# A decoder block with mLSTM and DeltaNet: all mLSTM queries and keys by seven-product blocks, DeltaNet columns projected in front, and mixer units of 40 steps

## The chip, the cores and the metric

The kernel runs on one core of a Trainium2 chip. The metric is the time of one execution on the device in microseconds (us), the median of three runs. Engines are called as the profile calls them: PE is TensorE (matrix products; PEld its weight loads), DVE VectorE, ACT ScalarE, POOL GpSimd, and SP SyncE, which here only issues DMAs.

## The reference

One layer on x of 512 rows and 2048 columns, float32. The input is normalised, one wide projection makes everything, two token mixers run side by side, and an output projection with a gated merge closes the layer:

```python
u = _rmsnorm(h, norm_w)
proj = jnp.matmul(u, w_in)            # to ml_q, ml_k, ml_v, ml_o, ml_z, ml_i, ml_f,
                                      # dn_qkv, dn_z, dn_b, dn_a, gate_a, gate_b
# mLSTM: 8 heads, query/key width 128, value width 256, chunkwise
h_a = _merge_heads(_rmsnorm(_mlstm_chunkwise(q, k, v, i_pre, logf))) * ml_norm_w
h_a = h_a * sigmoid(ml_o) * silu(ml_z)
# gated DeltaNet: 16 heads of 128; causal conv of 4 taps + SiLU on q, k, v
qkv = _causal_conv_silu(dn_qkv, dn_conv_w)
h_b = _merge_heads(_rmsnorm(_gated_delta_chunkwise(l2norm(dq), l2norm(dk), dv, beta, g), dn_norm_w)) * silu(dn_z)
y = sigmoid(gate_a) * (h_a @ w_out[:2048]) + sigmoid(gate_b) * (h_b @ w_out[2048:])
out = _rmsnorm(x + y)

# a chunk of DeltaNet, state S, gam the running sum of the log decay g
u = wv - wk @ S                       # wv, wk: solved from (I + strict(beta k k^T decay))
o = (q * exp(gam)) @ S + (q k^T * decay) @ u
S = exp(gam_end) * S + (k * exp(gam_end - gam))^T @ u
```

## The kernel before

Everything is float32. For a large product each operand is split in two reduced parts: ACT casts the upper part (`split_hi`, L140) and DVE subtracts it from the value (`split_lo`, L143). A product is then three matmuls: upper by upper, lower by upper, upper by lower (L257 to L259, L578 to L580). A weight tile is loaded by SP (`load_raw`, four buffers `wr`) and split into `wh` and `wl` (four buffers each).

PE's order is written by hand: instructions stand on each engine in the order in which the program issues them, moved only by the marks `urgent` (ahead) and `behind` (right after the newest split of that engine). The measure of progress is the step: after each group of six large matmuls `tick()` (L219) is called, and it resumes each of the generators that are due. A generator issues a piece of the mixers' work and gives back the number of steps after which it wants to go on (`yield 2`); `start(gen, wait)` sets its first step. So all times in the plan are counted in steps, not in us.

The stages are:

1. Front: the norm of x, its transposed split `uh`, `ul` in SBUF, gates, and four direct blocks (`proj_cm`, L246): 256 output columns, 16 row tiles, 96 matmuls, 16 steps. They make queries and keys of the first four mLSTM heads, which go to DRAM (`spill`).
2. The seven-product stage (`seven_stage`, L480): blocks of two times 512 columns by seven products of half size in place of eight, 336 matmuls each. Each block has half A (8 steps of four products) and half B (8 of three), where a product is a step. For a block DVE and ACT also form sums of weight tiles (L519, L520, L538) and split these. The list `SEVEN` has 13 blocks: mLSTM z and o gates, DeltaNet's gate, one block with the other four heads' queries and keys, mLSTM values, and the merge gates.
3. Eight mixer units (`dn_unit`, L1128) of 48 steps, two DeltaNet heads each. In a unit three direct blocks make the columns of keys, values and queries; each has a convolution (L828 to L837), SiLU (L843, L844) and a turn to token order (L860). Beside them run DeltaNet's generators: `dn_front_k` (key products and the decay matrix `dm`, L887, L898), `dn_front_q` (L985), `dn_back` (the triangular solve) and `dn_chain` (the recurrence over four chunks: pr, r, pw, w, pst, st, L1079 to L1102), and one mLSTM head (`ml_head`, L1161) whose first step is in `HEADS`.
4. The output projection: direct wide blocks, two seven-product blocks, a last block, and the final norm.

In `dn_chain` the value enters as v times beta (`vn` multiplied by `nk` on DVE, L1029), and the first product of a chunk, keys by state, is scaled by the negated decay `negeg` when r is formed:

```python
V.scalar_tensor_tensor(out=r, in0=pr, scalar=negeg[:, c, h:h + 1], in1=vn[:, c, :], op0=ALU.mult, op1=ALU.add)
```

The queries get the decay `eg` (in the tile `gb`) on POOL in `dn_front_q` (L995).

## Time and profile before

| | |
|---|---|
| median of three runs (lowest, highest) | 2144.73 us (2144.39, 2144.76) |
| the profiled execution, its span | 2143.23 us, 2141.5 us |
| mean granted TensorE clock | 0.998 |
| busy: PE, DVE, ACT, POOL | 99%, 80%, 49%, 21% |
| front with its four direct blocks | to 124 us |
| 13 seven-product blocks | 124 to 1115 us, some 76 us each |
| eight units | 1115 to some 1800 us, some 86 us each in the middle |
| output projection and final norm | the rest |

The span runs from the first to the last instruction. A busy PE is one that has a matmul in it; since matmuls are pipelined, a matmul's own length (0.39 us) is longer than the distance to the next. The line numbers (L257) are those of the kernel before.

### The profile page before, as it was taken

Reading aid. Unit: us, or ns where it says so; the run is one execution under the profiler, and the core shown is the slowest. Engines: PE = TensorE matmul, PEld = TensorE weight load, DVE = VectorE, ACT = ScalarE, POOL = GpSimd, SP = SyncE. Lnnn points to the kernel's source line nnn. Section 1 sums busy time; section 2 is a strip of 40 time slices with the busy share of each in tenths; the row PEclk is TensorE's granted clock in tenths of the full one; section 3 lists DMA queues with packets and bytes.
Section 4 is the critical chain, followed back from the end, with each engine's and each line's share of the span. In section 5 each row is a group of like instructions: output and inputs, shape, how many; then the busy total and the mean of one; then the engine's idle time right before and its main releaser. Section 6 shows DMA issues by size and latency. Waiting matters only on the chain.

```text
span 2141.5 us, 32018 instructions
## 1 busy us (share of the span) xinstructions
PE 2113.5 (99%) x10544; PEld 1752.6 (82%) x10544; DVE 1708.0 (80%) x2981; ACT 1057.6 (49%) x2066; POOL 451.1 (21%) x667
## 2 busy tenths in 40 slices
PE   6999999999999999999999999999999999999998
PEld 5888888888888888888888888888888888887886
DVE  5888888788788778777766887888878878569887
ACT  5444454445444444444445546456465464345345
POOL 0000000000004000000003335344343363233211
PEclk9999999999999999999999999999999999999999
DMA  5355676667677767766766867777686677778895
GB/s 162 119 192 190 212 217 198 220 199 224 206 234 237 245 196 226 240 209 212 253 205 165 208 166 180 183 180 192 182 211 173 171 189 224 196 223 287 245 302 225
DMA packets 447144, 444.21 MB, mean 207 GB/s; under 512 B 197121, under 2 KB 303842, under 8 KB 446850
## 3 DMA queue, kind: packets, MB, share of 16 engines
q1 hardware_dynamic: 377618, 337.22, 53.9%
q0 software_dynamic: 24752, 72.90, 10.9%
q10 hardware_dynamic: 44608, 32.06, 4.8%
q8 instruction: 82, 1.34, 0.3%
q14 instruction: 84, 0.69, 0.1%
HBM read 348.66 MB, written 97.58 MB: 208 GB/s over the span
## 4 chain that ended last, share of the span: by engine, by line
PE 95%; DVE 2%; DMA 2%; issue 1%; SPq 0%; POOL 0%; ACT 0%; DVEq 0%; POOLq 0%; ACTq 0%
PE ps L578 18%; PE ps L580 18%; PE ps L579 18%; PE pj L257 10%; PE pj L259 9%; PE pj L258 9%; PE py L1407 2%; PE py L1409 2%; PE py L1408 2%; PE pk L915 1%; DMA wr<-in_w_out_dram 1%; PE pqk L990 1%; PE pw L1087 1%; PE pnum L1213 1%; PE po L1102 1%
## 5 line engine op out<-in xcount | busy, mean ns | idle before, releaser
L143 DVE TENSOR_TENSOR wl<-wr,wh 128x512 fp32r<-128x512 f32 (+1 forms) x522 | 444.3, 852 | 176.5 <-ACT wh L140 172.3
L140 ACT CAST wh<-wr 128x512 fp32r<-128x512 f32 (+1 forms) x522 | 373.9, 717 | 422.1 <-PE pj L258 218.5
L257 PE MATMUL pj<-uh,wh 128*128 128x512 f32 x896 | 375.8, 419 | 0.0
L259 PE MATMUL pj<-uh,wl 128*128 128x512 f32 x896 | 351.5, 392 | 0.0
L258 PE MATMUL pj<-ul,wh 128*128 128x512 f32 x896 | 349.8, 390 | 0.0
L578 PE MATMUL ps<-wh,uh 128*128 128x512 f32 x752 | 292.7, 389 | 0.8 <-DVE X L632 0.8
L579 PE MATMUL ps<-wl,uh 128*128 128x512 f32 x752 | 292.6, 389 | 0.0
L580 PE MATMUL ps<-wh,ul 128*128 128x512 f32 x752 | 292.6, 389 | 0.0
L140 ACT CAST wh<-t 128x1024 fp32r<-128x1024 f32 x120 | 126.3, 1053 | 301.7 <-PE ps L580 197.5
L533 POOL DMA_DIRECT2D t_d<-ts x104 | 56.6, 544 | 921.8 <-DVE ts L520 853.5
L579 PE MATMUL ps<-wl,suh 128*128 128x512 f32 x624 | 242.9, 389 | 0.0
L580 PE MATMUL ps<-wh,sul 128*128 128x512 f32 x624 | 242.8, 389 | 0.0
L578 PE MATMUL ps<-wh,suh 128*128 128x512 f32 x624 | 242.8, 389 | 0.0
L140 ACT CAST wh<-ts 128x512 fp32r<-128x512 f32 x240 | 147.9, 616 | 184.7 <-DVE ts L538 157.6
L143 DVE TENSOR_TENSOR wl<-t,wh 128x1024 fp32r<-128x1024 f32 x120 | 147.0, 1225 | 81.9 <-ACT wh L140 81.5
L259 PEld LDWEIGHTS pj<-uh,wl 128*128 128x128 f32 x896 | 168.3, 188 | 37.0
L257 PEld LDWEIGHTS pj<-uh,wh 128*128 128x128 f32 x896 | 169.2, 189 | 29.7
L258 PEld LDWEIGHTS pj<-ul,wh 128*128 128x128 f32 x896 | 169.3, 189 | 28.5
L143 DVE TENSOR_TENSOR wl<-ts,wh 128x512 fp32r<-128x512 f32 x240 | 164.9, 687 | 32.6 <-ACT wh L140 31.2
L578 PEld LDWEIGHTS ps<-wh,uh 128*128 128x128 f32 x752 | 141.2, 188 | 30.4 <-DVE X L632 1.2
L579 PEld LDWEIGHTS ps<-wl,uh 128*128 128x128 f32 x752 | 141.2, 188 | 29.5
L580 PEld LDWEIGHTS ps<-wh,ul 128*128 128x128 f32 x752 | 141.2, 188 | 29.2
(345 smaller groups left out, 3804.2 us busy)
## 6 DMA issues: line engine op xcount, KB each, us to landing
wr<-in_w_in_dram SPq DMA_DIRECT2D x744, 256.0 KB, 3.6
wr<-in_w_out_dram SPq DMA_DIRECT2D x138, 256.0 KB, 4.8
t_d<-ts POOLq DMA_DIRECT2D x104, 256.0 KB, 3.6
wr<-t_d SPq DMA_DIRECT2D x104, 256.0 KB, 3.7
xt<-in_x_dram SPq DMA_DIRECT2D x8, 512.0 KB, 7.2
tg_d<-X ACTq DMA_DIRECT2D x16, 256.0 KB, 4.8
tg_d<-to ACTq DMA_DIRECT2D x16, 256.0 KB, 4.6
v<-v_d SPq DMA_DIRECT2D x8, 512.0 KB, 5.6
```

The costliest lines, as they stand in the source:

```text
L140: newest["A"] = A.copy(hi, src).ins
L143: newest["V"] = V.tensor_tensor(out=lo, in0=src, in1=hi.bitcast(F32), op=ALU.subtract).ins
L257: T.matmul(ps[j], hi[:, k, wsl], uh[:, kt, :], start=(kt == 0), stop=False)
L258: T.matmul(ps[j], hi[:, k, wsl], ul[:, kt, :], start=False, stop=False)
L259: T.matmul(ps[j], lo[:, k, wsl], uh[:, kt, :], start=False, stop=(kt == KT - 1))
L533: queue.dma_start(t2_d[b % 2, i], ts[:, 0, :])
L578: T.matmul(ps[t], ah, hi, start=(g == "A" and i == 0), stop=False, skip_group_check=True)
L579: T.matmul(ps[t], ah, lo, start=False, stop=False, skip_group_check=True)
L580: T.matmul(ps[t], al, hi, start=False, stop=(i == KH - 1), skip_group_check=True)
L1407: T.matmul(ps[c], uh[:, kt, tsl], hi, start=(kt == ks[0]), stop=False)
L1408: T.matmul(ps[c], uh[:, kt, tsl], lo, start=False, stop=False)
L1409: T.matmul(ps[c], ul[:, kt, tsl], hi, start=False, stop=(kt == ks[-1]))
```

## The change

The mLSTM queries and keys of all eight heads now come from two seven-product blocks (`SEVEN` has 14 blocks). The four direct blocks in front make DeltaNet columns instead: the keys of heads 0 and 1, and the values of the six odd heads 3 to 13, in pairs whose pieces of 128 columns lie 256 apart (kind "w", two DMAs per weight tile). Their raw results go to DRAM (`raw_d`). During the seven-product blocks 0 to 7, generators `before_mixers` read them back, one head each, and do convolution, SiLU and turn; the results go to DRAM once more (`pre_d`, `kc_d`).

So unit 0 has no key block (32 steps), units 1 to 6 project the values of one head only (`proj_half`, 8 steps; 40 in all), and unit 7 stays at 48: 320 steps in place of 384. `HEADS`, the waits of `dn_front_k` and `dn_back` and the start of `open_y` are set anew.

In DeltaNet, keys too are multiplied by `eg` on POOL after their own products are done; r is then formed in one instruction from v, beta and the product, and v is no more multiplied by beta ahead, but for chunk 0 (on ACT).

```diff
-HEADS = (1, 41, 85, 130, 178, 226, 274, 322)
+HEADS = (1, 37, 74, 111, 148, 186, 225, 264)
+PRE = (16, 17, 35, 37, 39, 41, 43, 45)
+VPRE = {(h - 33) // 2: i for i, h in enumerate(PRE) if h > 32}
 SEVEN = ([("z", ML_Z + c, ML_O + c) for c in range(0, D, NO)]
          + [("s", DN_Z + c, DN_Z + c + NO) for c in range(0, D, 2 * NO)]
-         + [("q", ML_Q + QKS, ML_K + QKS)]
+         + [("q", ML_Q, ML_K)]
          + [("v", ML_V + c, ML_V + c + NO) for c in range(0, D, 2 * NO)]
+         + [("q", ML_Q + NO, ML_K + NO)]
...
+    FRONT = [("i", DN_K)] + [("w", DN_V + (h - 32) * P) for h in PRE[2::2]]
+    plan = [(*f, k) for f in FRONT for k in range(0, KT, KP)]
     for p in UNITS:
-        for c in (DN_K, DN_V, DN_Q):
-            plan += [("i", c + p * NB, k) for k in range(0, KT, KP)]
+        for c in (DN_K, DN_V, DN_Q)[p == 0:]:
+            if c == DN_V and p in VPRE:
+                plan += [("h", c + p * NB, k) for k in range(0, KT, 2 * KP)]
+            else:
+                plan += [("i", c + p * NB, k) for k in range(0, KT, KP)]
...
+    def proj_half(col0):
+        ps = psj.tile([P, S], F32, tag="pj", name="pj")
+        for kt0 in range(0, KT, 2 * KP):
+            hi, lo = next_w("h", col0, kt0)
+            for k in range(2 * KP):
+                kt = kt0 + k
+                T.matmul(ps, hi[:, k, :], uh[:, kt, :], start=(kt == 0), stop=False)
+                T.matmul(ps, hi[:, k, :], ul[:, kt, :], start=False, stop=False)
+                T.matmul(ps, lo[:, k, :], uh[:, kt, :], start=False, stop=(kt == KT - 1))
+                if k % 2:
+                    tick()
+        return [ps]
...
             for n in range(N - 2):
+                if n == KH - 1 and beside:
+                    start(beside.pop(0))
...
+    def before_mixers(i):
+        raw = wp.tile([P, S], F32, tag="wr", name="pr0", bufs=NRAW)
+        with behind("S"):
+            nc.sync.dma_start(raw, raw_d[i])
+        yield 4
+        ct = PRE[i]
+        y = wp.tile([P, S], F32, tag="wr", name="py0", bufs=NRAW)
+        with behind("A"):
+            A.mul(y, raw, convc[:, 144 + ct:145 + ct])
+        for j in (2, 1, 0):
+            with behind("V"):
+                V.scalar_tensor_tensor(out=y[:, 3 - j:S], in0=raw[:, 0:S - 3 + j], scalar=convc[:, 48 * j + ct:48 * j + ct + 1],
+                                       in1=y[:, 3 - j:S], op0=ALU.mult, op1=ALU.add)
+            yield 1
+        with behind("A"):
+            A.activation(raw, y, AF.Tanh)
+        yield 1
+        with behind("V"):
+            V.scalar_tensor_tensor(out=y, in0=raw, scalar=1.0, in1=y, op0=ALU.add, op1=ALU.mult)
+        yield 1
+        with behind("V"):
+            V.transpose(raw, y)
+        if i < 2:
+            with behind("A"):
+                nc.scalar.dma_start(kc_d[i], y)
+        yield 2
+        ov = raw.rearrange("p (m c) -> p m c", c=BS)
+        for a in range(4):
+            with behind("A"):
+                nc.scalar.dma_start(pre_d[i, :, :, a, :].rearrange("m r c -> r m c"), ov[a * BS:(a + 1) * BS])
+            yield 1
...
-        yield 16
+        yield 11 if hs[0] // 2 in VPRE else 16
...
             G.tensor_tensor(out=qt, in0=qt, in1=eg, op=ALU.mult)
+            kt = kq[j][:, 0, :].rearrange("p (c t) -> p c t", t=P)
+            G.tensor_tensor(out=kt, in0=kt, in1=eg, op=ALU.mult)
...
-            with behind("V"):
-                V.tensor_tensor(out=vn, in0=vn, in1=bc(u["nk"][:, j, :], P), op=ALU.mult)
+            with behind("A"):
+                A.mul(vn[:, 0, :], vn[:, 0, :], u["nk"][:, j, 0:1])
...
-                    V.scalar_tensor_tensor(out=r, in0=pr, scalar=negeg[:, c, h:h + 1], in1=vn[:, c, :],
-                                           op0=ALU.mult, op1=ALU.add)
+                    V.scalar_tensor_tensor(out=r, in0=vn[:, c, :], scalar=u["nk"][:, j, c:c + 1], in1=pr,
+                                           op0=ALU.mult, op1=ALU.subtract)
...
-        ps = proj_cm(DN_K + dcol)
+        ps = proj_cm(DN_K + dcol) if p else None
...
+            else:
+                nc.sync.dma_start(kq[j][:, 0, :], kc_d[j])
+                start(turned(ke, j), 3 + j, front)
         start(dn_front_k(hs, kq, u), 1, front)
-        ps = proj_cm(DN_V + dcol)
+        ps = (proj_half if p in VPRE else proj_cm)(DN_V + dcol)
...
-        start(dn_back(hs, kq, u), 25 + 4 * last, by)
+        start(dn_back(hs, kq, u), 28 - (p == 0) + last, by)
...
-    start(open_y(), 200)
+    start(open_y(), 150)
```

Three places show how this moves the order. A row names the line (in the second of each pair a line of the changed kernel, where L143 is the cast and L146 the subtraction), the operation and the tiles.

ACT at the start of the units, before: casts of weight tiles, the first head's `wm`, and the first convolution (`yp`, `kq`); the exponentials of the decay matrix `dm` come further down.

```order
L140 CAST wh<-wr 128x512 x5
L1185 ACTIVATE wm<-wm,acol 128x128 x4
L140 CAST wh<-wr 128x512 x2
L828 COPY yp_9793<-pj 128x512
L835 ACTIVATE kq_9802<-yp_9793,convc 128x512
L140 CAST wh<-wr 128x512
```

The same place after the change:

```order
L143 CAST wh<-wr 128x512 x4
L961 ACTIVATE dm<-dm,ngam 128x128 x4
L966 ACTIVATE gb<-gb 128x512
L961 ACTIVATE dm<-dm,ngam 128x128 x4
L964 ACTIVATE dm<-gb,pgam 64x64
L143 CAST wh<-wr 128x512
L1257 ACTIVATE wm<-wm,acol 128x128 x4
L964 ACTIVATE dm<-gb,pgam 64x64 x3
L143 CAST wh<-wr 128x512
```

The exponentials of `dm` and of `gb` have moved in between two casts of weight tiles, after the eighth tile of the unit.

DVE in half B of the first seven-product block, before: wide subtractions (128x1024), thin ones (`ts`), and the sums of tiles (L538).

```order
L143 TENSOR_TENSOR wl<-wr_1451,wh 128x1024
L538 TENSOR_TENSOR ts<-wr_1489 128x512
L143 TENSOR_TENSOR wl<-wr_1489,wh 128x1024
L538 TENSOR_TENSOR ts<-wr_1535 128x512
L143 TENSOR_TENSOR wl<-ts,wh 128x512 x2
L143 TENSOR_TENSOR wl<-wr_1535,wh 128x1024
L538 TENSOR_TENSOR ts<-wr_1567 128x512
```

After the change, with the pieces of one head's convolution (L819), SiLU (L826) and turn (L829):

```order
L146 TENSOR_TENSOR wl<-wr_1512,wh 128x1024
L562 TENSOR_TENSOR ts<-wr_1560 128x512
L819 SCALAR_TENSOR_TENSOR py_1570<-pr_1524,convc,py_1570 128x510
L146 TENSOR_TENSOR wl<-ts,wh 128x512
L819 SCALAR_TENSOR_TENSOR py_1570<-pr_1524,convc,py_1570 128x509
L146 TENSOR_TENSOR wl<-ts,wh 128x512
L146 TENSOR_TENSOR wl<-wr_1560,wh 128x1024
L562 TENSOR_TENSOR ts<-wr_1597 128x512
L826 SCALAR_TENSOR_TENSOR py_1570<-pr_1524,py_1570 128x512
L829 STREAM_TRANSPOSE pr_1524<-py_1570 128x512
L146 TENSOR_TENSOR wl<-wr_1597,wh 128x1024
```

Five passes stand between the splits of three steps.

POOL in a unit, before: the queries' passes (`kq` by `gb`) with other work between.

```order
L995 TENSOR_TENSOR kq_10582<-kq_10582,gb 128x512
L887 AFFINE_SELECT dm<-gb 128x512
L1121 TENSOR_TENSOR rsd<-ssq,mhalf 128x4
L818 DMA gb<-rows_d 128x512
L1121 TENSOR_TENSOR rsd<-ssq,mhalf 128x4
L995 TENSOR_TENSOR kq_10583<-kq_10583,gb 128x512
L1122 TENSOR_TENSOR gz<-gz,rsd 128x512
```

After the change:

```order
L1058 TENSOR_TENSOR kq_11189<-kq_11189,gb 128x512
L1060 TENSOR_TENSOR kq_11189<-kq_11189,gb 128x512
L950 AFFINE_SELECT dm<-gb 128x512
L1058 TENSOR_TENSOR kq_11190<-kq_11190,gb 128x512
L1060 TENSOR_TENSOR kq_11190<-kq_11190,gb 128x512
L1259 COPY we<-wm 128x4
```

Each head's query pass is followed by a pass of the same size over the keys.

More of the change, by code (lines that the diff above doesn't have):

```diff
@@ L343, in first_block, with spill @@
             gate_products(kt - GLAG)
-    def spill(ps, o, scale, last=False):
+    def spill(ps, o, last=False):
         for j in range(2):
@@ L777, in hybrid_body @@
             "z": sink_z, "s": sink_s}
+    def before_mixers(i):
[29 more added lines that the diff above has]
+            yield 1
+    ahead = [before_mixers(i) for i in range(len(PRE))]
     def begin_mixers():
@@ L782, in begin_mixers @@
         prepare(nfront - 1)
-    lead, seven = seven_stage(sbp, (suh, sul), (s4h, s4l), X, t2_d, w_in, 0, SEVEN, SINK, begin_mixers, G)
+    lead, seven = seven_stage(sbp, (suh, sul), (s4h, s4l), X, t2_d, w_in, 0, SEVEN, SINK, begin_mixers, G, ahead)
     start(gates())
@@ L789, in hybrid_body @@
     start(lead(), 38)
-    for a, b in QK[1:]:
-        spill(proj_cm((ML_Q, ML_K)[a] + b * NB), 2 * QKFIRST * a + 2 * b, 1.0 if a else float(P) ** -0.5, (a, b) == QK[-1])
+    for i, (kind, c) in enumerate(FRONT[1:]):
+        spill(proj_cm(c, kind=kind), 2 * i + 2, i == len(FRONT) - 2)
     for b, blk in enumerate(SEVEN):
@@ L1126, in dn_chain, with turned @@
         turn(g, h_d[h], G if soon else nc.scalar, 3 if soon else 5)
+    def turned(dst, i):
+        with behind("S"):
+            nc.sync.dma_start(dst, pre_d[i].rearrange("(n j) r a c -> (j r) n (a c)", n=NC))
+        yield 1
     def dn_unit(p):
@@ L1145, in dn_unit @@
             u["vs"].append(vt)
-            conv_silu(ps[j], 32 + hs[j], vt.rearrange("p c t -> p (c t)"))
-            start(silu_end(vt.rearrange("p c t -> p (c t)"), (vt, vt)), 4 + 3 * j, front)
+            if j < len(ps):
+                conv_silu(ps[j], 32 + hs[j], vt.rearrange("p c t -> p (c t)"))
+                start(silu_end(vt.rearrange("p c t -> p (c t)"), (vt, vt)), 4 + 3 * j, front)
+            else:
+                start(turned(vt, VPRE[p]), 6, front)
         if last:
```

64 lines of the change are left out of this document (32 added, 32 removed).

## The prediction

> **What bounds the kernel now.** I read the busy times of the page first, then the chain of work that ended last, then the waits of TensorE.
>
> ```profile
> PE 2113.5 (99%) x10544; PEld 1752.6 (82%) x10544; DVE 1708.0 (80%) x2981; ACT 1057.6 (49%) x2066; POOL 451.1 (21%) x667
> ...
> PE 95%; DVE 2%; DMA 2%; issue 1%; SPq 0%; POOL 0%; ACT 0%; DVEq 0%; POOLq 0%; ACTq 0%
> ...
> PE pprm L108 <- POOL rs L304: 14.6, 1, 14.6
> PE put L313 <- DVE xt L290: 2.1, 2, 1.3
> PE ps L578 <- DVE X L632: 0.8, 1, 0.8
> PE ps L578 <- DVE X L1431: 0.7, 2, 0.5
> PE pw L1087 <- DVE r L1082: 0.3, 1, 0.3
> ```
>
> PE is busy 99% of the span and carries 95% of the chain. It waited seven times, 18.5 us in all, of which 16.7 lie at the start (the lines of the input norm) that the change leaves alone. So the time is the number of matmuls on PE times what one takes, plus a start and an end. Whatever else the change does counts only if it makes PE wait, and in the whole seven-product stage and the units PE hardly ever does.
>
> What a matmul takes, and how the stages stand (each row: the stretch, then busy us of PE, PEld, DVE, ACT, POOL with counts, clock, DMA share, GB/s):
>
> ```profile
> 124.00:581.00 457.00, 457.00 (x2017) 378.28 (x2016) 378.61 (x487) 216.69 (x311) 25.36 (x47) 1.00 0.66 210
> 1399.00:1485.00 86.00, 86.00 (x530) 72.02 (x529) 70.62 (x178) 48.29 (x135) 36.26 (x50) 1.00 0.73 184
> 1571.00:1657.00 86.00, 86.00 (x529) 71.94 (x529) 70.39 (x178) 47.97 (x135) 35.58 (x49) 1.00 0.76 192
> ```
>
> In the seven-product stage 2017 matmuls filled 457 us without a gap: 457 / 2017 = 0.2266 us each at the granted clock of 1.00 (a matmul's own row says 0.39 us, but they are pipelined). A unit of 48 steps takes 86 us, in which DVE is busy 70.5 us (82%), ACT 48 and POOL 36.
>
> **The change part by part.** *Matmuls.* A block of 256 columns by the direct way has 96 matmuls (16 row tiles, two halves, three products); a seven-product block has 336 and does the work of four direct ones. Before, there are 4 direct blocks in front, 24 in the units and 13 + 2 seven-product blocks: 28 x 96 = 2688 and 15 x 336 = 5040. After, there are 4 in front, and in the units 2 in unit 0, 2.5 in each of units 1 to 6 and 3 in unit 7, which is 24 x 96 = 2304; and 16 x 336 = 5376. The rows of the instruction order bear this out: PE's list shrinks by 48. 48 x 0.2266 = **-10.9 us**. By stage: the seven-product stage grows by 336 x 0.2266 = 76.1 us, units 1 to 6 shrink by 48 x 0.2266 = 10.9 us each to 75.1, unit 0 by 21.8. DeltaNet's and the heads' small matmuls keep their number, so nothing is earned there.
>
> *The units, 40 steps instead of 48.* The helpers must do a unit's work in 75.1 us.
>
> ```profile
> L143 DVE TENSOR_TENSOR wl<-wr,wh 128x512 fp32r<-128x512 f32 x96 | 76.3, 795 | 25.5 <-ACT wh L140 25.3
> L837 DVE SCALAR_TENSOR_TENSOR vt<-yp,convc,vt 128x512 f32<-128x512 f32 x24 | 18.1, 767 | 0.0
> L860 DVE STREAM_TRANSPOSE to<-vt 128x512 f32<-128x512 f32 x8 | 5.6, 703 | 0.0
> L844 DVE SCALAR_TENSOR_TENSOR vt<-th,vt 128x512 f32<-128x512 f32 x8 | 5.4, 679 | 0.0
> L1029 DVE TENSOR_TENSOR vt<-vt,nk 128x512 f32<-128x512 f32 x8 | 5.1, 685 | 0.0
> ...
> L995 POOL TENSOR_TENSOR kq<-kq,gb 128x512 f32<-128x512 f32 x8 | 10.3, 1286 | 0.1
> ...
> ACT wh L140 <- PE pj L258: 95.9, 65, 3.1
> ```
>
> (Four units together, 1399 to 1743 us.) DVE loses 4 tile splits x 0.795, the convolution, silu and turn of one head's values (3 x 0.767 + 0.679 + 0.703) and two passes of values by beta (2 x 0.685): 8.2 us. That leaves 70.5 - 8.2 = 62.3 of 75.1 us, 83% where it was 82%. The multiplication that those two passes did goes into the one instruction that forms r, which is there before and after. ACT loses four casts and a conv multiply or two and gains two 128x128 multiplies, and stays near 60%. POOL gains two passes x 1.286 and comes to 38.6 of 75.1, 51%. No engine but PE gets near its unit. The work that covers this is the reserve of split tiles: there are four split buffers, and 65 of the 96 casts of these four units waited for PE to release one (the last row), so that three whole tiles of 12 matmuls, 8.2 us, stand ready when a cast starts. Cost 0 in the sum for engines' load.
>
> Chains are another matter. Between two steps there are 6 large matmuls (1.36 us) and whatever small ones fall in, and DeltaNet's chain goes PE, ACT or DVE, PE from one step to the second next. With 40 steps a unit's same chain is laid over fewer steps, so more chains stand side by side, and in the order I find a handful of places where one of the three small PSUM banks is asked for again after 1.6 to 1.8 us. The nearest row is pw waiting 0.3 us for r, the dearest of its kind 0.8 us. From below: the one wait of 0.3 us goes, -0.3. From above: one wait of 0.8 us in each of eight units, +6.4. I take **+1.0**, nearer the low end, because chains of this length cost 0.3 us in eight units before.
>
> *From the seven-product stage into unit 0.* Here something new stands ahead of a weight cast. Unit 0 has no key block any more, its keys are read back, and so the decay matrix is asked for 17 steps earlier. In ACT's list its exponentials now stand between the cast of the eighth weight tile and that of the ninth; before they came four casts later, when the stage was long under way.
>
> ```profile
> 1124.62 0.96 POOL L811 MEMSET tb<- 128x1024 f32 x1 [8.26 <-DMA wr<-in_w_in_dram]
> ...
> 1127.04 1.07 POOL L818 DMA_DIRECT2D gb<-rows_d  x2
> ...
> 1132.94 0.62 POOL L887 TENSOR_SCALAR_AFFINE_SELECT dm<-gb 128x512 f32<-128x512 f32 x1 [0.94 <-DMA gb<-rows_d]
> ...
> 1114.84 0.39 PE L257 MATMUL pj<-uh,wh 128*128 128x512 f32 x1
> ...
> 1128.41 0.62 ACT L140 CAST wh<-wr 128x512 fp32r<-128x512 f32 x1 [2.10 <-PE pj L258]
> 1131.14 1.28 ACT L1185 ACTIVATE wm<-wm,acol 128x128 f32<-128x128 f32 x4 [2.11 <-POOL wm L1180]
> ...
> 1146.70 1.27 ACT L898 ACTIVATE dm<-dm,ngam 128x128 f32<-128x128 f32 x4
> ...
> 1147.88 0.62 ACT L903 ACTIVATE gb<-gb 128x512 f32<-128x512 f32 x1
> ...
> 1148.84 1.05 PE L915 MATMUL pk<-kq 128*128 128x128 f32 x8
> ```
>
> In this profile's clock: POOL's first work of the stage starts at 1124.62, held by a transfer; the decay's row is fetched at 1127.04 and the masked matrix is there at about 1132.9 + 0.6; in the new order POOL issues that fetch about 1 us earlier, so ACT gets the first matrix near 1132.6. Then come two groups of four exponentials (1.27 each), one pass of 128x512 (0.62) and the wait for POOL's second matrix: the ninth cast ends near 1136.5 and its subtraction near 1137.3, where the old cast in this place began at 1128.41. PE starts the stage at 1114.84 and asks for the ninth tile after 8 x 12 x 0.2266 = 21.8 us and three groups of small products (two of pk and one of the first head; some 0.9 us each by the last row, 1.05 to the end of its eight records), at 1139.3. That is 2.0 us to spare. From below 0; from above the fetch of the row takes twice its 5.9 us (1127.04 to 1132.94), and PE waits 5.9 - 2.0 = +3.9. I take **+0.5**.
>
> *The work put beside the seven-product stage.* Eight pieces go into blocks 0 to 7, each in the second half, where PE reads wide tiles.
>
> ```profile
> 557.20 1.23 DVE L143 TENSOR_TENSOR wl<-wr,wh 128x1024 fp32r<-128x1024 f32 x1 [0.87 <-ACT wh L140]
> 558.35 0.68 DVE L538 TENSOR_TENSOR ts<-wr 128x512 f32<-128x512 f32 x1
> 559.72 0.69 DVE L143 TENSOR_TENSOR wl<-ts,wh 128x512 fp32r<-128x512 f32 x1 [0.69 <-ACT wh L140]
> 561.28 1.23 DVE L143 TENSOR_TENSOR wl<-wr,wh 128x1024 fp32r<-128x1024 f32 x1 [0.87 <-ACT wh L140]
> ...
> 560.20 1.05 ACT L140 CAST wh<-wr 128x1024 fp32r<-128x1024 f32 x1 [0.52 <-PE ps L580]
> ...
> 561.54 0.39 PE L579 MATMUL ps<-wl,uh 128*128 128x512 f32 x1
> ```
>
> A step there is 4.08 us (557.20 to 561.28), in which DVE idles 0.87 + 0.69 = 1.56 us, for ACT casts that in turn wait for PE to release a buffer (the ACT row). A piece gives DVE three conv passes, one silu pass and a turn: 3 x 0.767 + 0.679 + 0.703 = 3.7 us, laid over three steps, so 1.2 us a step into 1.56 us of idle. The wide split that ended at 558.43 is read by PE at 561.54, 3.1 us later. Three passes that fall in one step make that 2.1, and the next two steps catch it up. From below 0, since PE waits nowhere there; from above the whole 3.7 less 3.1, 0.6 us in eight blocks, +5. I take **0**. What covers it is those 3.1 us; if they are gone, the price is that of the pieces, 30 us at most.
>
> *Front, transfers, tail.* The front has the same 4 blocks; its new kind of tile is fetched by two issues instead of one. SP issues one in 0.6 us (the SP row) against 2.7 us of matmuls per tile, and the stretch's share of the DMA engines is low:
>
> ```profile
> 1127.09 0.60 SPq L172 DMA_DIRECT2D wr<-in_w_in_dram  x1
> ...
> 45.00:110.00 65.00, 65.00 (x306) 52.53 (x305) 49.61 (x109) 27.30 (x52) 0.61 (x2) 1.00 0.40 118
> 657.00:1114.00 457.00, 457.00 (x2018) 378.47 (x2017) 357.20 (x448) 206.33 (x291) 44.53 (x83) 1.00 0.69 223
> ...
> DMA packets 447144, 444.21 MB, mean 207 GB/s; under 512 B 197121, under 2 KB 303842, under 8 KB 446850
> ```
>
> The results stored once more and the sums of one more seven-product block add some 9 MB (10 and 8 tiles of 0.26 MB, written and read) to the 444 MB. In a unit the per-unit transfers now fall in 75.1 us: 0.75 of the engines for 86 us becomes at most 0.75 x 86 / 75.1 = 0.86, less four tiles. The tail's products and waits (the ps rows with X) keep their order. All **0**.
>
> *Sum.* 2143.23 (profiled execution: its span of 2141.5 and 1.7 around it) - 10.9 + 1.0 + 0.5 = 2133.8. The profiled execution lies 1.5 us under the median of 2144.73, so against that median **2135.3 us**.
>
> **A rule against the change.** One row shows DVE held by POOL:
>
> ```profile
> 1465.99 2.01 DVE L143 TENSOR_TENSOR wl<-wr,wh 128x512 fp32r<-128x512 f32 x1 [1.41 <-ACT wh L140]
> ...
> 1465.15 1.31 POOL L995 TENSOR_TENSOR kq<-kq,gb 128x512 f32<-128x512 f32 x1
> 1466.40 1.05 POOL L1122 TENSOR_TENSOR gz<-gz,rsd 128x512 f32<-128x512 f32 x1
> ```
>
> A split of 0.69 us took 2.01 while POOL ran two passes end to end, until 1467.45. The change makes such a run longer by 1.29 us, twice a unit. Held every time, DVE loses 2 x 1.29 = 2.6 us a unit, 64.9 of 75.1, and the 8.2 us of split tiles cover one hold of 5 us. The Trainium skill ("SBUF — State Buffer", section "Who interferes with whom") says that a DVE instruction with two SBUF inputs and a GpSimd instruction that reads SBUF contend, and that the later one blocks fully; the 2.01 us agrees with it. By the skill the sum changes only where the held DVE instruction stands in a chain of a step.
>
> **Rivals.**
> 1. *The gain is given back in short waits* (no change). All upper bounds above that are of PSUM loops, transition and seven-product steps come in by a half to two thirds: 6.4 + 3.9 + 5 = 15.3, of which 7 to 10. On 2144.73 - 10.9 = 2133.8 that is 2141 to 2144. For it: PE's order is fixed, so that every miss is paid in full, and the number of places is large. Against it: before, the same kind of order cost 1.8 us from the start to the end.
> 2. *DVE's idle time in a unit is latency, not slack* (slower). In a unit DVE idles 86 - 70.5 = 15.5 us. If all of that comes back in 40 steps, a unit takes 62.3 + 15.5 = 77.8 instead of 75.1, 2.7 x 6 = 16.2 us more: 2133.8 + 16.2 = 2150. If POOL's longer holds come on top, 2.6 x 6 more, 2165. It decides once the chains of a unit need over 75.1 us and PE's lead of 8.2 us is used up in the first three units. For it: 83% busy with chains is high, and the holds are real. Against it: 25.3 of DVE's idle in four units is waiting for casts, which wait for PE, so it is slack behind PE.
> 3. *Nothing is lost at all*, 2133.8 less the 0.3 and part of the 1.5 us of waits in the tail: about 2132.5. This I count to the forecast.
>
> That the change does not do what it says is out: the counts are in the order.
>
> **How the numbers follow.** Forecast with rival 3: 0.77. Rival 1: 0.14. Rival 2: 0.09. Three runs of this kernel lie within 0.4 us, and 0.2% (4.3 us) is about what can be told from no change: faster is below 2140.4, slower above 2149.0. So faster 0.77, same 0.14, slower 0.09. The forecast's own range is 2132 to 2139 (the costs from -0.5 to +5). For the 8 in 10 I go from 2131.5 into rival 1, to 2142.
>
> **What would show it.** In the waits of PE: few rows and under 5 us outside the start; in the matmul groups 768 of each of the three pj lines instead of 896; seven-product windows of 457 us with about 2017 matmuls and DVE near 83% of them plus 3.7 us a block; units 1 to 6 of 75 us with DVE near 62. Rival 1 would show rows of PE waiting for ACT or DVE in the units, or ps waiting for wl in the blocks' second halves. Rival 2 would show units of 77 us and more with pj waiting for wl. The transition is judged by the first pj rows after the last seven-product block: a wait for the ninth tile's wl. The forecast is wrong if PE's waits outside the start exceed 7 us, or if the clock falls under 1.00.

## The result and the profile after

| | before | the change |
|---|---|---|
| median | 2144.56 us (2143.84 to 2144.76) | 2192.50 us (2188.53 to 2193.30) |
| ratio, 95% interval | | 1.0217 (1.0205 to 1.0230) |
| profiled execution, its span | 2143.23, 2141.5 us | 2192.21, 2190.4 us |
| mean granted TensorE clock | 0.998 | 0.994 |

The change makes the kernel 48 us slower, where the prediction had it 9 us faster. Against the count of matmuls (2133.8 us, the time before less 10.9) 59 us are lost. The page of the changed kernel, its busy times and its chain by engine (line numbers are those of the changed kernel):

```profile
PE 2121.5 (97%) x10496; PEld 1748.6 (80%) x10496; DVE 1758.8 (80%) x3010; ACT 1068.1 (49%) x2087; POOL 484.2 (22%) x723
...
PE 71%; DVE 9%; DMA 9%; issue 5%; ACT 2%; POOL 2%; SPq 1%; ACTq 0%; DVEq 0%; POOLq 0%
```

48 matmuls fewer, as counted; but PE's part of the chain fell from 95% to 71%. DVE's share of the span is the same 80% as before, so this column alone shows nothing. The waits of PE do (what waited, for what; us in total, times, longest):

```profile
PE pprm L111 <- POOL rs L331: 14.6, 1, 14.6
PE pr L1144 <- DVE st L1163: 7.2, 5, 2.6
PE pw L1152 <- DVE r L1147: 5.9, 4, 2.4
PE pst L1159 <- DVE tmp L1027: 3.8, 1, 3.8
PE pk L978 <- DVE kq L907: 3.7, 1, 3.7
PE py L1479 <- ACT wh L143: 2.9, 3, 1.7
PE p L1085 <- DVE tn L1045: 2.8, 2, 2.5
PE pj L286 <- DVE wl L146: 2.6, 1, 2.6
```

These are the largest of 23 rows; before there were five. Outside the start (the rows pprm and put) PE waits 42.3 us where it waited 1.8, and the prediction called itself wrong above 7. Most of them wait for DVE. Of the 36.2 us that lie in the units, 31.8 stand before DeltaNet's small products: pr (keys by state, waiting for the state st), pw (waiting for r), pst, pk and p. Weight splits (wl) make 4.3 us in all. Where the time lies is read from PE's timeline at the borders of the stages: the first product of the units (1114.84 before, in the prediction's rows), the first of the output projection (py), and the last of all.

```profile
1785.66 0.48 PE L1407 MATMUL py<-wh,uh 128*128 128x512 f32 x1
...
2131.70 0.39 PE L1409 MATMUL py<-wh,ul 128*128 128x512 f32 x1
```

And of the changed kernel, with three windows (span, then busy us and instructions of PE, PEld, DVE, ACT and POOL, granted clock, DMA share, GB/s):

```profile
1191.16 0.39 PE L284 MATMUL pj<-uh,wh 128*128 128x512 f32 x1
...
1824.59 0.47 PE L1479 MATMUL py<-wh,uh 128*128 128x512 f32 x1
...
2180.76 0.39 PE L1481 MATMUL py<-wh,ul 128*128 128x512 f32 x1
...
124.00:1190.00 1066.00, 1066.00 (x4703) 882.31 (x4702) 887.00 (x1139) 499.74 (x712) 102.57 (x182) 1.00 0.70 223
...
1191.20:1824.60 633.40, 596.79 (x3610) 491.59 (x3608) 501.80 (x1252) 344.62 (x973) 278.30 (x389) 0.99 0.70 178
...
1282.64:1777.71 495.07, 466.33 (x2897) 384.71 (x2896) 398.16 (x1000) 269.80 (x790) 220.14 (x312) 0.99 0.69 175
```

| stretch | before | by the count | the change | lost |
|---|---|---|---|---|
| to the first product of the units | 1114.84 | 1114.84 + 76.14 | 1191.16 | 0.2 |
| units | 670.82 | 670.82 - 384 x 0.2266 = 583.81 | 633.43 | 49.6 |
| output projection, first to last product | 346.04 | 346.04 | 356.17 | 10.1 |

The work beside the seven-product stage costs nothing (PE 1066.00 of 1066 us). The loss is in the units: PE idles for 633.40 - 596.79 = 36.6 of the 49.6 us (28.7 of them in units 1 to 6, the third window). Of the other 13.0 at most 6.8 are matmuls at half clock (see the clock at the end); the rest is not accounted for. Units 1 to 6, each taken from its first key product to that of the next, last 80.3 to 85.9 us where 75.1 were worked out, and DVE is busy 398.16 / 6 = 66.4 us in one where 62.3 were worked out. A part of the loss is in the output projection, whose first block runs beside the last unit's chain: there PE waits 4.6 us for weight casts and splits (py and ps for wh and wl), which it did not before.

One correction to the description of the kernel: only PE's list follows the program's order. The lists of DVE, ACT, POOL and SP are made by a planner from the data dependences and the marks, so that a pass written later in the program may stand where it stood. In the experiments steps are therefore moved by moving PE's part of them.

### The profile page after: what moved, and what is told of

Read it like the earlier page. It is cut to its first block, busy times and chain, and to the rows that moved or that the text cites. A ratio compares the mean times of both kernels' runs of the same rounds, so it can differ in the third digit from the quotient of the medians.

```text
span 2190.4 us, 32199 instructions
## 1 busy us (share of the span) xinstructions
PE 2121.5 (97%) x10496; PEld 1748.6 (80%) x10496; DVE 1758.8 (80%) x3010; ACT 1068.1 (49%) x2087; POOL 484.2 (22%) x723
## 4 chain that ended last, share of the span: by engine, by line
PE 71%; DVE 9%; DMA 9%; issue 5%; ACT 2%; POOL 2%; SPq 1%; ACTq 0%; DVEq 0%; POOLq 0%
PE ps L603 17%; PE ps L602 17%; PE ps L604 17%; PE pj L284 4%; PE pj L285 4%; PE pj L286 3%; DVE wl L146 2%; DMA y_d<-ty 1%; DVE xi L1029 1%; PE py L1479 1%; PE py L1480 1%; PE py L1481 1%; DMA ls<-ld 1%; DVE tmp L1027 1%; DVE kq L900 1%
## 5 line engine op out<-in xcount | busy, mean ns | idle before, releaser
L146 DVE TENSOR_TENSOR wl<-wr,wh 128x512 fp32r<-128x512 f32 (+1 forms) x506 | 431.1, 853 | 163.4 <-ACT wh L143 155.6
L143 ACT CAST wh<-wr 128x512 fp32r<-128x512 f32 (+1 forms) x506 | 367.6, 727 | 389.3 <-PE pj L285 149.2
L602 PE MATMUL ps<-wh,uh 128*128 128x512 f32 x800 | 311.4, 389 | 0.8 <-DVE X L658 0.8
L603 PE MATMUL ps<-wl,uh 128*128 128x512 f32 x800 | 311.3, 389 | 0.0
L604 PE MATMUL ps<-wh,ul 128*128 128x512 f32 x800 | 311.2, 389 | 0.0
L143 ACT CAST wh<-t 128x1024 fp32r<-128x1024 f32 x128 | 134.9, 1054 | 317.5 <-PE ps L604 213.9
L284 PE MATMUL pj<-uh,wh 128*128 128x512 f32 x672 | 284.7, 424 | 0.9 <-ACT yp L891 0.9
L286 PE MATMUL pj<-uh,wl 128*128 128x512 f32 x672 | 265.3, 395 | 2.6 <-DVE wl L146 2.6
L285 PE MATMUL pj<-ul,wh 128*128 128x512 f32 x672 | 263.7, 392 | 0.0
L603 PE MATMUL ps<-wl,suh 128*128 128x512 f32 x672 | 261.5, 389 | 0.0
L143 ACT CAST wh<-ts 128x512 fp32r<-128x512 f32 x256 | 158.1, 618 | 182.5 <-DVE ts L562 154.9
L146 DVE TENSOR_TENSOR wl<-t,wh 128x1024 fp32r<-128x1024 f32 x128 | 156.7, 1224 | 84.4 <-ACT wh L143 83.9
L146 DVE TENSOR_TENSOR wl<-ts,wh 128x512 fp32r<-128x512 f32 x256 | 175.2, 685 | 24.4 <-ACT wh L143 23.0
L602 PEld LDWEIGHTS ps<-wh,uh 128*128 128x128 f32 x800 | 150.1, 188 | 32.5 <-DVE X L658 1.2
L543 DVE TENSOR_TENSOR t<-wr 128x1024 f32<-128x1024 f32 x128 | 156.0, 1219 | 6.3 <-DMA wr<-in_w_in_dram 3.5
L286 PEld LDWEIGHTS pj<-uh,wl 128*128 128x128 f32 x672 | 126.9, 189 | 31.3 <-DVE wl L146 3.0
L603 PEld LDWEIGHTS ps<-wl,suh 128*128 128x128 f32 x672 | 126.2, 188 | 26.5 <-DVE wl L146 0.4
```

The costliest lines, as they stand in the source:

```text
L143: newest["A"] = A.copy(hi, src).ins
L146: newest["V"] = V.tensor_tensor(out=lo, in0=src, in1=hi.bitcast(F32), op=ALU.subtract).ins
L284: T.matmul(ps[j], hi[:, k, wsl], uh[:, kt, :], start=(kt == 0), stop=False)
L285: T.matmul(ps[j], hi[:, k, wsl], ul[:, kt, :], start=False, stop=False)
L286: T.matmul(ps[j], lo[:, k, wsl], uh[:, kt, :], start=False, stop=(kt == KT - 1))
L543: V.tensor_tensor(out=t13, in0=r[:, 1:3, :], in1=r[:, 0:2, :], op=ALU.subtract)
```

## The experiments

Three theories were set up on what delays r and st on DVE. **Holds**: POOL's passes over queries and keys now fall into the triangular solve (62 short instructions per unit, `tmp` and `xi`, each needing the one before) and hold it. **Burst** (called squeeze at first, for the 40 steps as such): the solve now lies on the same steps as the query convolutions, the chain and the passes. In the 48-step plan the solve lay on steps -8 to 7 of the next unit and the query passes came at steps 9 and 10; with 40 steps it lies on steps 0 to 15, and the passes stayed at 9 and 10. **Load** (or "passes", for POOL alone): it is the amount of work, wherever it stands. The row on which the first rests is this, of the changed kernel, DVE, then POOL, then PE:

```profile
1338.66 0.68 DVE L1056 TENSOR_TENSOR aq<-pqk,dm 128x512 f32<-128x512 f32 x1
1339.26 6.40 DVE L1029 TENSOR_TENSOR xi<-xi,tmp 128x72 f32<-128x72 f32 x1
1345.69 0.23 DVE L1027 TENSOR_TENSOR tmp<-ls,xi 128x68 f32<-128x68 f32 x1
...
1339.96 1.30 POOL L1058 TENSOR_TENSOR kq<-kq,gb 128x512 f32<-128x512 f32 x1
1341.21 1.29 POOL L1060 TENSOR_TENSOR kq<-kq,gb 128x512 f32<-128x512 f32 x1
1342.46 0.63 POOL L950 TENSOR_SCALAR_AFFINE_SELECT dm<-gb 128x512 f32<-128x512 f32 x1
1343.07 1.28 POOL L1058 TENSOR_TENSOR kq<-kq,gb 128x512 f32<-128x512 f32 x1
1344.31 1.26 POOL L1060 TENSOR_TENSOR kq<-kq,gb 128x512 f32<-128x512 f32 x1
...
1344.30 0.40 PE L286 MATMUL pj<-uh,wl 128*128 128x512 f32 x1
1348.53 0.46 PE L1159 MATMUL pst<-w,ke 128*128 128x128 f32 x2 [3.83 <-DVE tmp L1027]
```

An instruction of 0.24 us took 6.40, until POOL's fourth pass ended; what was queued behind it on DVE came 6 us late, and PE stood for 3.83 us.

### The DeltaNet part, alone and undone

Undone in the change (e1), and alone in the kernel before (e2):

```diff
-            G.tensor_tensor(out=kt, in0=kt, in1=eg, op=ALU.mult)
...
-                A.mul(vn[:, 0, :], vn[:, 0, :], u["nk"][:, j, 0:1])
+                V.tensor_tensor(out=vn, in0=vn, in1=bc(u["nk"][:, j, :], P), op=ALU.mult)
...
+                    V.scalar_tensor_tensor(out=r, in0=pr, scalar=negeg[:, c, h:h + 1], in1=vn[:, c, :], ...
```

> The change without its DeltaNet part: keys get no decay on POOL, v is again multiplied by beta on DVE, r is formed as before; front, seven-product stage and 40-step units as in the change. Theory 'holds' (POOL's passes over queries and keys now run while DVE is in the triangular solve, and hold its short instructions for up to 6 us): about half of what the query and key passes hold (35 us in the changed kernel's units) goes, 2165 to 2178 us. Theory 'squeeze' (40 steps are too short for DVE's chains, whatever POOL does): no gain, since DVE gets 1.4 us a unit more, 2188 to 2200. Theory 'passes' (it is the number of passes on POOL, wherever they stand): 2137 to 2145.

Measured 2173.9 us, 1.0136 (1.0121 to 1.0151): 18.6 us back, within the range of "holds" and of no other, with 40.1 still lost.

> The kernel before with the DeltaNet part of the change alone: keys get their decay on POOL right behind the queries, v is no more multiplied by beta on DVE, r is formed in the new way; units of 48 steps. Theory 'holds': the solve is over when POOL's passes start in these units, so 2143 to 2149 us. Theory 'squeeze': the same, 2142 to 2147. Theory 'passes': 16 passes of 1.29 us cost about themselves, 2158 to 2170.

Measured 2149.2 us, 1.0019 (1.0009 to 1.0028), 0.2 us above the range of "holds". In 48-step units the same passes cost 4.4 us for the whole DeltaNet part, not the 16 x 1.29 of "passes".

### The passes later, and left out

```diff
-        start(dn_front_q(hs, kq, u), QWAIT + 3 * last, by)
+        start(dn_front_q(hs, kq, u), QWAIT + 3 * last + 8 * (p in VPRE), by)
```

> The changed kernel with one number changed: in the six units of 40 steps the query part (products of queries and keys, then POOL's passes over both) starts 8 steps later, at step 17 of the next unit, after the solve instead of within it. Theory 'holds': PE's waits for r, st and pst go with the holds, 2138 to 2160 us. Theory 'squeeze': 2185 to 2195. Theory 'passes': 2185 to 2195.

Measured 2183.7 us, 1.0178 (1.0163 to 1.0193): 8.8 us back, a miss of all three. For e4 POOL's passes over queries and over keys were both left out:

```diff
-            G.tensor_tensor(out=qt, in0=qt, in1=eg, op=ALU.mult)
-            kt = kq[j][:, 0, :].rearrange("p (c t) -> p c t", t=P)
-            G.tensor_tensor(out=kt, in0=kt, in1=eg, op=ALU.mult)
```

> The changed kernel with POOL's two passes per head left out (neither queries nor keys get their decay, so this part of the computation is missing). Theory 'holds': 2138 to 2160 us. Theory 'squeeze': 2180 to 2195, since DVE's chains are as long as before. Theory 'passes': 2137 to 2150.

Measured 2176.9 us, 1.0148 (1.0131 to 1.0165), again a miss of all three. Without any of these passes 43 of 59 us are still lost. So these passes, with whatever they hold, are about a quarter of it; the row above was the most striking, not the typical one. What e4 still waits for stands in its trace:

```profile
1555.34 0.19 DVE L1027 TENSOR_TENSOR tmp<-ls,xi 128x31 f32<-128x31 f32 x1 [8.02 <-DMA ls<-ld]
...
1559.51 0.28 DVE L1160 COPY st<-pst 128x128 f32<-128x128 f32 x1
...
1559.85 0.80 PE L1141 MATMUL pr<-st,kq 128*128 128x128 f32 x2 [5.45 <-DVE st L1160]
```

DVE stands 8.02 us at the first instruction of the solve, whose input `ls` comes through DRAM and has not landed. The copy of the state stands behind it in DVE's list, and so PE stands 5.45 us for st. In all DVE stands 20.7 us for `ls` in e4 and 17.1 in the change, where it stood 5.9 before; the solve's own instructions take 116.0 us in e4, about what they took before (114.2). So the solve is not held here; a transfer lands later than the plan of steps allows for, and what makes it late is not shown. In the change itself, waits for st of 1.48 and 2.41 us follow such stands of 4.09 and 4.67 us. And e1, which keeps the query passes, is 3.0 us faster than e4, which has none: the rest of the DeltaNet part (vn's multiply on ACT, the other form of r) is not free either.

### Units of 48 steps on the changed front

```diff
-VPRE = {(h - 33) // 2: i for i, h in enumerate(PRE) if h > 32}
+VPRE = {}
...
-HEADS = (1, 37, 74, 111, 148, 186, 225, 264)
+HEADS = (1, 37, 74, 114, 162, 210, 258, 306)
...
-        start(dn_back(hs, kq, u), 28 - (p == 0) + last, by)
+        start(dn_back(hs, kq, u), 25 + 2 * (p == 0) + 4 * last, by)
```

> The changed front and seven-product stage, without the DeltaNet part (keys get no decay on POOL), but units 1 to 6 project both value heads again, so they have 48 steps with the old waits; the six values made ahead are not used. That is 288 matmuls more than the change: 2133.8 + 288 x 0.2266 = 2199.1 without any wait. Theories 'burst' and 'load' both: the stalls in the units go, what stays is the entry into unit 0 (4 to 7 us), 2202 to 2208. Rival 'front' (the work made ahead, its transfers or the new places of the heads cost the time): 2225 to 2240.

Measured 2205.3 us, 1.0282 (1.0267 to 1.0298), within the range of "burst" and "load" and 6.2 over its count of matmuls. The run to set beside it is e1, also without the DeltaNet part, which with 40 steps loses 40.1. The waits of PE in it, outside the start, are that of the entry and some of 1.0 us or less, for instance:

```profile
PE pj L286 <- DVE wl L146: 2.6, 1, 2.6
...
PE pnum L1288 <- DVE xi L1032: 1.0, 1, 1.0
...
PE pw L1153 <- DVE r L1148: 0.4, 1, 0.4
```

This is the clearest of all: the new front, the work made ahead and the heads' places cost 6.2 us together, the entry included. Most of the loss comes with the 40 steps and what goes with them (e6 does not read the six values made ahead back into the units, so their last transfer is not in it).

### The entry into unit 0

```diff
-        start(dn_front_k(hs, kq, u), 1, front)
+        start(dn_front_k(hs, kq, u), 1 if p else 4, front)
```

> The changed kernel with DeltaNet's key part of unit 0 started 3 steps later, so that the exponentials of the decay matrix no longer stand ahead of the ninth weight cast. If the entry into unit 0 costs what its waits show (2.8 us for wl, 1.1 for a freed PSUM bank, 1.0 later, and half a clock for 3.4 us): 2184 to 2188. If the wait only moves: 2190 to 2194.

Measured 2193.3 us, 1.0218 (1.0201 to 1.0235). The wait of pj for wl at the entry is gone from the trace, but the time is the same; as I read it, what is won at the entry is lost again as long as later steps wait for DVE. On the best version so far (e8, below) the same edit does count:

> e8_kqv (2154.7 us) with the key part of unit 0 started 3 steps later, as in e7_entry_late. If the entry's waits (2.8 + 1.1 + 1.1 us) were covered there by later stalls and are not now: 2148 to 2151. If the wait only moves: 2153 to 2157.

Measured 2150.3 us, 1.0025 (1.0015 to 1.0035), 4.4 less than e8.

### The places of the solve in 48-step units

First the solve 8 steps later in the kernel before, with the wait behind it shortened by as much:

```diff
-        yield 9
+        yield 17
         for i in range(BS - 1):
...
-        yield 16
+        yield 8
```

> The kernel before, units of 48 steps, with the triangular solve started 8 steps later (and the wait behind it 8 steps shorter): as in the 40-step units, the solve now falls on the first 16 steps of the next unit, together with the query convolutions and POOL's query passes. Theory 'burst' (what costs is that the solve, the convolutions, the chain's small steps and POOL's passes fall on the same steps of DVE): 2153 to 2172 us. Theory 'load' (DVE has too little time over the whole 40-step unit): nothing is added to the unit, 2143 to 2148.

Measured 2251.9 us, 1.0499 (1.0483 to 1.0515), far above both ranges. This is no test of "burst": PE waited 87.9 us for tn alone, the solve's result after its way through DRAM, for which 8 steps are too few. The places of the change itself are 17, 11 and 28:

```diff
-        yield 9
+        yield 17
...
-        yield 16
+        yield 11
...
-        start(dn_back(hs, kq, u), 25 + 4 * last, by)
+        start(dn_back(hs, kq, u), 28 + 4 * last, by)
```

> The kernel before, units of 48 steps and no other part of the change, with the places that the solve has in the change's 40-step units: the solve 8 steps later (on the first 16 steps of the next unit), 11 steps from its end to the turned inverse, the back part from step 28 on (it was 25). DVE's, POOL's and ACT's work is that of the kernel before. Theory 'burst' (the solve on the same steps as the query convolutions, POOL's query passes and the chain): 2150 to 2170 us, with PE waits for r, st and tn in the units. Theory 'load' (too little DVE time in a 40-step unit): 2143 to 2148.

Measured 2174.4 us, 1.0134 (1.0117 to 1.0151). Just over the range of "burst", but not for its reason. PE's waits in it, and then what DVE waited for in the units:

```profile
PE p L1020 <- DVE tn L982: 16.4, 6, 4.2
...
DVE tn L982 <- DMA tt<-xd: 19.8, 7, 5.5
```

No wait for r or st; it is the transfer again, which has 11 steps here where it had 16. So in this plan the solve beside the query convolutions does not delay r and st. What it shows is that the plan of before has less room than that: the solve 8 steps later, and what follows it 3, lose 30 us over eight units of 48 steps.

### The order keys, queries, values

On e1: in units 1 to 6 the query block stands before the half value block, and the query products and POOL's query passes come after the solve.

```diff
-        for c in (DN_K, DN_V, DN_Q)[p == 0:]:
+        for c in (DN_K, DN_Q, DN_V) if p in VPRE else (DN_K, DN_V, DN_Q)[p == 0:]:
...
+            start(dn_q_norms(u), 20, by)
+            start(dn_front_q(hs, kq, u), 23, by)
```

> The changed kernel without the DeltaNet part (as e1_kt_undone, 2173.9 us), and in units 1 to 6 the blocks in the order keys, queries, values: the convolutions of the queries (two heads) come before the solve, in it only those of one value head; POOL's query passes come after the solve. Theory 'burst': most of the 34 us of waits go, 2142 to 2160. Theory 'load': DVE's work in the unit is the same, 2168 to 2178.

Measured 2154.7 us, 1.0048 (1.0033 to 1.0063): 19.2 us back with the same work, within the range of "burst". "Load" is out, the places matter. But then the same with the DeltaNet part back in (the edit of e1 reversed):

> The whole change, the DeltaNet part on POOL too, with the block order keys, queries, values of e8_kqv (2154.7 us without the DeltaNet part). Theory 'burst': POOL's two passes per head now come after the solve, so the key passes cost about what they did in 48-step units (4.4 us), 2156 to 2164. Theory 'load': their price stays the 18.6 us that e1_kt_undone showed, 2170 to 2177.

Measured 2187.2 us, 1.0196 (1.0181 to 1.0211): the DeltaNet part costs 32.5 us here, though its key passes come after the solve. Both theories missed. PE's waits for DVE are back:

```profile
PE pw L1159 <- DVE r L1154: 8.1, 3, 3.2
PE pcs L1311 <- DVE aq L1056: 3.9, 1, 3.9
PE pw L1159 <- DVE aq L1056: 3.8, 2, 3.0
```

### Passes and chain apart

A last theory: passes cost when the **chain** of the unit before is running (steps -4 to 20 with 40 steps, -15 to 9 with 48). Two runs move the passes past the chain, on e11, without and with the DeltaNet part (e12, e13); two move the chain over the passes in the kernel before, likewise (e14, e15):

```diff
-            start(dn_front_q(hs, kq, u), 23, by)
+            start(dn_front_q(hs, kq, u), 29, by)
...
-        start(dn_back(hs, kq, u), 25 + 4 * last, by)
+        start(dn_back(hs, kq, u), 31 - 2 * last, by)
```

> e11_kqv_entry (2150.3 us, no key passes) with the query products and POOL's query passes 6 steps later, at steps 21 and 22 of the next unit, when the chain of the unit before (steps -4 to 20) is over. Theory 'chain': 2140 to 2148 us. Theory 'tight': 2148 to 2153.

> e12_kqv_q21 with the key passes on POOL, so the whole change with other places of its steps. Theory 'chain': the key passes cost 0 to 6 us over e12_kqv_q21. Theory 'tight': 15 to 35 us over it, as in the change and in e10_kqv_kt.

> The kernel before with DeltaNet's back part 6 steps later (31 for 25; in the last unit 29), so that the chain lies on steps -9 to 15 of a unit and POOL's query passes (steps 9 and 10) fall within it. Theory 'chain': the two query passes hold r and st, 2147 to 2160 us. Theory 'tight': 2143 to 2148.

> e2_kt_alone (2149.2 us: the kernel before with the key passes on POOL) with the back part 6 steps later as in e14_back_late. Theory 'chain': the key passes cost 12 to 30 us over e14_back_late, where they cost 4.4 without the chain beside them. Theory 'tight': 3 to 6 us over it.

Measured, in this order: 2164.6 us (1.0093, 1.0077 to 1.0108), 2186.8 (1.0195, 1.0178 to 1.0211), 2159.5 (1.0074, 1.0057 to 1.0090) and 2161.1 (1.0074, 1.0057 to 1.0090). e12 lies 12 us above both ranges; e13, 22.2 us over e12, is within that of "tight" (the passes cost in any unit of 40 steps); e14 is within that of "chain"; e15, 1.6 us over e14, which is no difference that shows, is below both. So the DeltaNet part costs 22.2 us in 40-step units with the chain away and next to nothing in 48-step units with the chain beside it, and "chain" does not explain its price. Nor is e14 the hold of r and st that "chain" foretold: its PE waits 6.0 us for s, a step of the back part, 0.2 for st and nothing for r. "Tight" fits the price of the DeltaNet part, missed e12 and e14, and names no cause. In e13 DVE stands 25.4 us for `ls`, against 7.6 in e12 (2.1 in e10 and 3.1 in e8): the late transfer of e4 comes back with the DeltaNet part in one order of blocks and place of the passes, and not in the other. Moving a step costs by itself too: 14.3 us for the query products 6 steps later (e12 against e11), 14.6 for the back part 6 steps later.

### The query passes on DVE

On e11 the query passes go from POOL to DVE; e17 has the products 3 steps earlier as well (23 to 20), and e18, on e16, the passes over ke on DVE too.

```diff
-            G.tensor_tensor(out=qt, in0=qt, in1=eg, op=ALU.mult)
+            with behind("V"):
+                V.tensor_tensor(out=qt, in0=qt, in1=eg, op=ALU.mult)
...
-            G.tensor_tensor(out=ke, in0=ke, in1=bc(u["dm"][j][0][:, :, P - 1], P), op=ALU.mult)
+            with behind("V"):
+                V.tensor_tensor(out=ke, in0=ke, in1=bc(u["dm"][j][0][:, :, P - 1], P), op=ALU.mult)
```

> e11_kqv_entry (2150.3 us) with the query passes on DVE instead of POOL: DVE does 2 x 0.69 us a unit more, and POOL's 15.5 us of holds during these passes go. If holds are what is left: 2141 to 2147 us. If the places of the steps are what is left: 2149 to 2155.

> e16_kqv_qdve with the query products and passes 3 steps earlier (step 12 of the next unit instead of 15), away from the key convolutions and into the solve. If the key convolutions beside them cost: 2 to 5 us less than e16_kqv_qdve. If the solve beside them costs: 2 to 15 us more.

Measured 2143.0 us, 0.9990 (0.9981 to 0.9999), within the range of "holds", and 2144.1 us, 0.9995 (0.9985 to 1.0004), outside both ranges. Taking the query passes from POOL gives 7.2 us (e16 against e11); the 3 steps between the two make no difference that shows. e16 is the best version found: hardly faster than before, by 0.2 to 4.1 us of the 10.9 that the matmuls give. It has the changed front and 40-step units, the new block order, the entry 3 steps later and no DeltaNet part. Taken one after another, the DeltaNet part left out (18.6 us, e1), the block order (19.2, e8), the entry (4.4, e11) and the query passes on DVE (7.2, e16) lead from 2192.5 to 2143.0 us; 9.2 of the 58.7 us are left. The solve's instructions by group, before, in the change and in e16 (busy us, mean ns):

```profile
L964 DVE TENSOR_TENSOR tmp<-ls,xi 128x60 f32<-128x60 f32 (+24 forms) x248 | 61.1, 246 | 13.7 <-DMA ls<-ld 5.9 <-DMA td<-to 3.7
L966 DVE TENSOR_TENSOR xi<-xi,tmp 128x60 f32<-128x60 f32 (+24 forms) x248 | 53.1, 214 | 5.7
```

```profile
L1029 DVE TENSOR_TENSOR xi<-xi,tmp 128x60 f32<-128x60 f32 (+24 forms) x248 | 76.2, 307 | 4.7
L1027 DVE TENSOR_TENSOR tmp<-ls,xi 128x60 f32<-128x60 f32 (+24 forms) x248 | 73.2, 295 | 21.7 <-DMA ls<-ld 17.1
```

```profile
L1030 DVE TENSOR_TENSOR tmp<-ls,xi 128x60 f32<-128x60 f32 (+24 forms) x248 | 60.1, 242 | 5.1 <-DMA td<-to 0.4
L1032 DVE TENSOR_TENSOR xi<-xi,tmp 128x60 f32<-128x60 f32 (+24 forms) x248 | 56.9, 229 | 4.8
```

The same instructions took 149 us in the change where they took 114 before and 117 in e16; and at their head DVE stood 17.1 us for the solve's input (`ls`, through DRAM) where it stood 5.9 before.

> e16_kqv_qdve (2143.0 us) with the passes over ke (keys scaled to the end of the chunk, two of 128x512 a unit) on DVE as well: DVE does 1.4 us a unit more, and the 11 us of holds during them go. If holds are still the price: 2137 to 2141 us. If DVE's own time is it by now: 2143 to 2148.

Measured 2164.9 us, 1.0093 (1.0076 to 1.0109): 22 us worse, a miss of both. PE's two largest waits after the start, and what DVE waited for behind them:

```profile
PE p L1095 <- DVE nk L989: 12.5, 2, 8.7
PE p L1095 <- DVE tn L1049: 6.0, 3, 4.0
...
DVE tn L1049 <- DMA tt<-xd: 17.4, 5, 5.0
```

DVE stands 17.4 us at tn for the solve's result on its way through DRAM, where it stood 2.6 in e16, and nk is queued behind tn (the longest of PE's waits ends 0.6 us after such a stand of 4.96 us). Why the pass over ke on DVE makes this transfer later is not shown.

## Why the prediction was wrong

**What held.** The count of matmuls and the term of -10.9 us: the units start at 1191.2 us, 76.3 later than before, against 76.1 worked out. So held the terms of 0 for the front and for the work beside the seven-product stage.

**The entry** went another way than forecast. From the timelines of ACT, DVE and PE of the changed kernel:

```profile
1211.56 1.26 ACT L961 ACTIVATE dm<-dm,ngam 128x128 f32<-128x128 f32 x4
...
1213.21 0.62 ACT L143 CAST wh<-wr 128x512 fp32r<-128x512 f32 x1
...
1223.24 4.39 DVE L900 SCALAR_TENSOR_TENSOR vt<-yp,convc,vt 128x512 f32<-128x512 f32 x3 [2.58 <-ACT vt L898]
1227.56 1.28 DVE L146 TENSOR_TENSOR wl<-wr,wh 128x512 fp32r<-128x512 f32 x2
...
1228.29 0.50 PE L286 MATMUL pj<-uh,wl 128*128 128x512 f32 x1 [2.60 <-DVE wl L146]
```

The ninth cast was expected near 1136.5, which is 1212.8 on this clock; it ran to 1213.83, 1.0 us later, and PE did not wait for it. The wait of 2.6 us came at 1228.29, some 13 us later, for a split that stood on DVE behind convolution passes, which stood behind ACT (2.58 us). The bound of +3.9 had looked at one tile only. With the decay 3 steps later the time falls by 4.4 us in the plan of e8 (e11), where the term was +0.5.

**The step that failed** is the term for the chains, "Chains are another matter", taken as +1.0 with an upper bound of 6.4. It measured 49.6 us in the units, less what of the entry falls in them. (The tail, put at 0, lost 10.1.) Two things in it were wrong. The bound was made from a long wait of the kernel before, 0.8 us a unit; that row is a wait of ps for X, outside the units, and not of the chain's kind. But a plan whose waits are near zero does not say how much room it has; that PE waited 1.8 us before meant only that each distance in steps sufficed. e9 and e14 show how little was over: the solve 8 steps later and the back part 6 steps later cost 30 and 15 us in units of the old length. And I compared DVE's busy share of a whole unit (83% for 82%), though the unit's steps are not alike: the query convolutions, the solve, the chain and POOL's passes share some 20 steps of it. The share itself came out at about 80% (66.4 of 82.5 us), because the units grew with it.

"Cost 0 in the sum for engines' load", covered by three split tiles or 8.2 us, held for the splits themselves: PE waited for wl 2.6 us in all the units, at the entry. It does not cover r, st, tn or pk, which have no buffer in front of PE and are asked for one or two steps after they start.

**The rivals.** Rival 2 (DVE's idle time is latency, not slack) was right in direction and in its sign that units grow over 77 us (80.3 to 85.9), and had 0.09; its price of 2150 to 2165 us was too low, because it took DVE's idle time of before as the most that can come back, and left out the clock (below). Its own sign, "pj waiting for wl", did not show; the waits are at the chain. Its ground for being unlikely, that 25.3 us of the idle time stand behind PE, was true and beside the point. Rival 1 had the mechanism of many short waits, at 7 to 10 us of their 59.

**The rule weighed there** (the Trainium skill, "SBUF — State Buffer", section "Who interferes with whom") agrees with the 6.40 us row in that DVE's instruction ends with POOL's fourth pass. By the rows DVE's instruction starts first, at 1339.26 against 1339.96, so which came later is not settled by them. The 7.2 us between e11 and e16 go the rule's way. The prediction let it change the sum only where a held instruction stands in a chain; part of the case lay in this sentence, and I did not look which of DVE's instructions stand beside POOL's passes once the solve has moved by 8 steps. The order of the changed kernel could have told.

**What stays open.** That most of the loss belongs to the 40 steps is shown (e6 against e1), and that it depends on where steps stand (e8, e9, e14) and on POOL's passes (e4, e16). Why DVE stands so long for `ls` in the change, e1, e4 and e13 is open; no run moved that transfer alone. Why the DeltaNet part costs 18.6, 32.5 and 22.2 us in three plans of 40 steps and 4.4 and 1.6 in two of 48 is not settled: it costs so with its passes in the solve, behind it, and past the chain, and its passes were not run apart from the other form of r and ACT's multiply. The 8 us that e16 still loses against its count of matmuls are nearly all in its trace: 7.9 us of short waits of PE, none over 0.9 us, beside those that the kernel before has too; no run took them away.

## What to carry to other kernels

Where a plan is counted in steps of the bounding engine, shortening the period moves everything that is counted from another block's end against everything counted from its own; write down which steps of the helpers coincide before and after, not their share of the period. A plan without waits has unknown slack, and the cheapest way to learn it is one run that moves a late step by a few steps. Price chains by what is asked for within a step of its start, since the buffers of the bulk operands do not cover them.
